# Banded attention: the sink as one more column of the logits, and every second block's result in a bank of the projections

## The chip, the cores and the metric

The kernel runs on one core of a Trainium2 chip. The metric is the device time of one execution in microseconds (us). The engines of the core work side by side, each through its own queue in order, and wait for one another by semaphores: TensorE (PE, with its weight loads as PEld), VectorE (DVE), ScalarE (ACT), GpSimd (POOL) and SyncE (SP), which here issues the DMAs.

## The reference, cut to what matters

The program is a trunk of four residual layers: a gated convolution, forgetting attention, gated DeltaNet, and sliding-window attention with sinks. Only the last one is touched. It has 16 query heads of 64 in 4 groups, a window of 128 tokens, and for every head one learned sink that takes part in the softmax and has no value:

```python
s = einsum('bnqhgd,bnkhd->bnhgqk', qb, kk) / sqrt(d)     # a block of 128 queries, 256 keys
logits = where(mask, s, -inf)
m = maximum(max(logits, -1), sink)
e = exp(logits - m)
p = e / (sum(e, -1) + exp(sink - m))
o = einsum('bnhgqk,bnkhd->bnqhgd', p, vv)
return (o * silu(z)) @ w_out
```

## The kernel before

Everything is float32, and the products are made of a high and a low part (`hi`, `lo`), so that a projection of 128 columns by 512 tokens is 8 times 3 matmuls (`proj_steps`, L158 to L160) into one PSUM bank.

PSUM has eight banks, given out by `psum(tag)`: three that rotate under the tag "pj" (each new tile takes the next of the three, and waits until the readers of the tile before it in that bank are through), two under "tr", two under "sc" and one under "ov".

`layer_swa` runs the attention as 64 blocks: 8 groups g (two heads each) times 8 blocks i of 128 queries; block n is g = n // 8, i = n % 8. TensorE's order is written out by hand (`manual_schedule`); the other engines' orders come from the scheduler. In step n of the loop TensorE does the logits of block n (`ps_sc`), the transposes of block n - 2 (`ps_tr`, L1164) and the product with the values of block n - 3 (L1173, `ps_ov`, 4 matmuls), and between these three it is filled with projections for the next group (`window`, `slot`): queries in two halves, the gate in two halves, and in group 3 also keys. So about two steps carry one projection. In group 7 the filling is the output projection.

One block (`swa_block`) goes through the engines like this:

- DVE, twice: logits plus band mask, with a running minimum that starts at the negated sink (L1150; logits are kept negated, so the minimum is the negated maximum).
- ACT, twice: exponential with its sum (L1153).
- The sink: DVE adds minimum and sink (L1155), ACT takes the exponential (L1156), DVE adds it to the sums (L1157). All three are on tiles of 128 by 2.
- DVE: reciprocal (L1158); POOL: logits times reciprocal (L1159).
- PE: transposes (L1164); ACT: high part `phi` (L1167); DVE: low part `plo` (L1168).
- PE: values (L1173) into `ps_ov`; ACT copies two quarters of it (L1177, L1178), DVE adds the other two (L1179, L1180), which frees the bank; DVE multiplies into `y` (L1183).

A projection's bank is freed by its readers: for queries by the copy `ra` on ACT (L957), after which SP swaps halves of heads by four DMAs into `acc` (L960), POOL and DVE rotate (L961 to L963), and ACT and DVE split the result into `qst` (L1012, L1017, L1019); for a gate by a tanh on ACT (L289) and the product on DVE (L290).

Of the kernel before, what the change touches and what calls it, by code (L numbers as in the profile page):

```python
# [21 lines left out]
P = 128  # L22
# [23 lines left out]
class Core:  # L46
# [286 lines left out]
    def start(self, layer, wsrc, st):  # L333
# [33 lines left out]
        def arrive(half, c):  # L367
            if c >= NC_:
                return
            if c not in pts[half]:  # L370
                pts[half][c] = self.psum("sc", 2) if c % 3 < 2 else self.psum("ov")
                for b in range(4):
                    turn(half, b, c)
            nc.scalar.copy(self.Y[c][half], pts[half][c])

        with self.tc.manual_schedule(engines={E.PE, E.Activation, E.DVE}):
# [16 lines left out]
            self.pre = [[self.split_w(raw, P, nc.vector) for raw in raws[:2]]]  # L393
            for c in range(1, AHEAD):
                arrive(0, c)
            self.pre.append([self.split_w(raw, P) for raw in raws[2:3]])
            for half in range(NH):
                lows = []
                for c in range(NC_ + 1):
                    if c < NC_:  # L400
# [530 lines left out]
def layer_swa(k, out):  # L931
    nc = k.nc
    w_in = k.a["swa_w_in"][0]
    with k.tc.tile_pool(name="sw", bufs=1) as p:
        tab = [[p.tile([P, HT], F32, name=f"rt{j}_{h}") for h in range(NH)] for j in range(2)]
        for h in range(NH):
            for j in range(2):
                nc.sync.dma_start(out=tab[j][h], in_=k.rope[j][h])
        sk = p.tile([P, 2, 16], F32, name="sk")
        nc.sync.dma_start(out=sk[:, 0, :], in_=k.a["swa_sinks"][0].partition_broadcast(P))  # L940
        nc.vector.tensor_scalar(sk[:, 1, :], sk[:, 0, :], -1.0, None, op0=ALU.mult)

        band = p.tile([P, 2 * P], F32, name="band")
        nc.gpsimd.memset(band, 0.0)
# [22 lines left out]
        vv = [p.tile([P, 4, P], F32R, name=f"vv{b}") for b in range(8)]  # L967
# [104 lines left out]
        with k.tc.manual_schedule(engines={mybir.EngineType.PE}):  # L1072
# [20 lines left out]
            for n in range(64 + 4):  # L1093
                g, i = n // 8, n % 8
# [29 lines left out]
def swa_block(k, p, g, i, q, kk, vv, sk, band):  # L1124

    nc = k.nc
    kv = g // 2
    qsl = slice((i % 4) * P, (i % 4 + 1) * P)
    kbs = [i - 1, i] if i else [0]
    n = len(kbs) * P  # L1130
    ps = k.psum("sc", 2).rearrange("p (u n) -> p u n", u=2)
    lg = p.tile([P, HT], F32, name="lg", bufs=3).rearrange("p (u n) -> p u n", u=2)
    st = k.small.tile([P, 4, 2], F32, name="st", bufs=6)

    runs = []
    for kb in kbs:
        if runs and runs[-1][0] == kb // 4:
            runs[-1][2] += P
        else:
            runs.append([kb // 4, (kb % 4) * P, P])  # L1140
    for u in range(2):
        at = 0
        for h, k0, w in runs:
            kh, kl = kk[g // 4, h]
            nc.tensor.matmul(ps[:, u, at:at + w], q[u][:, qsl], kh[kv % 2][:, k0:k0 + w], start=True, stop=False)
            nc.tensor.matmul(ps[:, u, at:at + w], q[u][:, qsl], kl[kv % 2][:, k0:k0 + w], start=False, stop=True)  # L1146
            at += w
    for u in range(2):
        hd = 2 * g + u
        nc.vector.tensor_tensor_reduce(lg[:, u, :n], ps[:, u, :n], band[:, 2 * P - n:], 1.0, sk[:, 1, hd:hd + 1],  # L1150
                                       ALU.add, ALU.min, st[:, 0, u:u + 1])
    for u in range(2):
        nc.scalar.activation(lg[:, u, :n], lg[:, u, :n], AF.Exp, bias=st[:, 0, u:u + 1], scale=-1.0,  # L1153
                             accum_out=st[:, 1, u:u + 1])
    nc.vector.tensor_tensor(st[:, 2, :], st[:, 0, :], sk[:, 0, 2 * g:2 * g + 2], op=ALU.add)  # L1155
    nc.scalar.activation(st[:, 2, :], st[:, 2, :], AF.Exp)  # L1156
    nc.vector.tensor_tensor(st[:, 2, :], st[:, 2, :], st[:, 1, :], op=ALU.add)  # L1157
    nc.vector.reciprocal(st[:, 3, :], st[:, 2, :])  # L1158
    nc.gpsimd.tensor_tensor(lg[:, :, :n], lg[:, :, :n], st[:, 3, :].unsqueeze(2).broadcast_to([P, 2, n]), op=ALU.mult)  # L1159
    yield  # L1160
    pt = k.psum("tr")
    for j in range(len(kbs)):
        for u in range(2):
            nc.tensor.transpose(pt[:, (2 * j + u) * P:(2 * j + u + 1) * P], lg[:, u, j * P:(j + 1) * P], k.ident)  # L1164
    hi = p.tile([P, HT], F32R, name="phi", bufs=2)
    lo = p.tile([P, HT], F32R, name="plo", bufs=2)
    nc.scalar.copy(hi[:, :2 * n], pt[:, :2 * n])  # L1167
    nc.vector.tensor_tensor(lo[:, :2 * n], pt[:, :2 * n], hi[:, :2 * n].bitcast(F32), op=ALU.subtract)  # L1168
    yield
    ov = k.psum("ov")  # L1170
    for j, kb in enumerate(kbs):
        for x in (hi, lo):
            nc.tensor.matmul(ov[:, :256], vv[kb][:, kv, :], x[:, j * 256:(j + 1) * 256],  # L1173
                             start=(j == 0 and x is hi), stop=(j == len(kbs) - 1 and x is lo))

    o = p.tile([P, P], F32, name="o", bufs=3)
    nc.scalar.copy(o[0:64, 0:P], ov[64:128, 0:P])  # L1177
    k.mark = nc.scalar.copy(o[64:128, 0:P], ov[0:64, P:2 * P])  # L1178
    nc.vector.tensor_tensor(o[0:64, 0:P], ov[0:64, 0:P], o[0:64, 0:P], op=ALU.add)  # L1179
    nc.vector.tensor_tensor(o[64:128, 0:P], ov[64:128, P:2 * P], o[64:128, 0:P], op=ALU.add)  # L1180
    yield
    y = k.Y[g][i // 4][:, qsl]
    nc.vector.tensor_tensor(y, y, o[:, 0:P], op=ALU.mult)  # L1183
    yield "end"


class Gdn:
# [146 lines left out]
    def decay(self, hd, h):  # L1334
# [111 lines left out]
    def loads(self, hd, h):  # L1446
# [9 lines left out]
        for q in range(4):  # L1456
# [429 lines left out]
```

## Time and profile before

| | us |
|---|---|
| median of 3 runs | 2175.01 (2165.24 to 2175.88) |
| the profiled execution | 2172.09 |
| its span on the core | 2170.4 |
| TensorE busy in the span | 2086.8 (96%) |
| VectorE busy | 1347.4 (62%) |
| ScalarE busy | 993.1 (46%) |
| GpSimd busy | 838.4 (39%) |

The shares are means over four layers with different limits. The blocks of the attention run from about 1735 to 2090 us of the span; what the change is worth is read there. A busy TensorE may be busy at half its clock: the granted clock stands beside it in the view by stretches.

### The profile page before, as it was taken

The numbers are of one execution on the slowest core, as the hardware profiler recorded it, in microseconds if no ns is written. First come the engines' busy times: TensorE is split into PE (matmuls) and PEld (weight loads), VectorE is DVE, ScalarE is ACT, GpSimd is POOL, SyncE is SP. The second block draws the span as 40 slices with busy tenths as digits, with TensorE's granted clock in tenths as the row PEclk, the third lists the DMA queues.
The fourth block names the chain that finished last, engine by engine and source line by source line (L and its number), as shares of the span: only waits on it lengthen the run. The fifth ranks groups of instructions, "written<-read, shape, count | busy, mean of one in ns | idle before, by whom it ended". The sixth has DMA issues, their size and how long they took to land.

```text
span 2170.4 us, 33535 instructions
## 1 busy us (share of the span) xinstructions
PE 2086.8 (96%) x11717; PEld 1753.5 (81%) x11717; DVE 1347.4 (62%) x2876; ACT 993.1 (46%) x2483; POOL 838.4 (39%) x721
## 2 busy tenths in 40 slices
PE   7999999999999999999999799999999998998898
PEld 6887888788988989888687677888887797877788
DVE  8647645544535353655456967765557658898874
ACT  6333334424333343543365444343444356666664
POOL 2344445631212212236366643223326544453630
PEclk9999999999999999999999999999999999999999
DMA  6122215731222312136266453333316421111134
GB/s 234 49 73 88 58 54 160 212 62 50 40 40 40 49 43 42 49 123 181 64 188 185 136 167 104 85 110 91 102 56 199 141 65 38 44 52 40 44 91 143
DMA packets 288367, 205.71 MB, mean 95 GB/s; under 512 B 41381, under 2 KB 245574, under 8 KB 288198
## 3 DMA queue, kind: packets, MB, share of 16 engines
q1 hardware_dynamic: 288198, 203.56, 33.4%
q8 instruction: 93, 1.52, 0.3%
q14 instruction: 76, 0.62, 0.1%
HBM read 154.87 MB, written 43.38 MB: 91 GB/s over the span
## 4 chain that ended last, share of the span: by engine, by line
PE 71%; DVE 14%; DMA 5%; issue 4%; ACT 3%; POOL 2%; SPq 1%; ACTq 0%; POOLq 0%; DVEq 0%
PE ps_pj L158 14%; PE ps_pj L159 14%; PE ps_pj L160 14%; PE ps_sc L247 2%; PE ps_sc L249 2%; PE ps_sc L248 2%; DVE sp L1428 1%; PE ps_tr L834 1%; DVE cu L1307 1%; PE ps_pj L247 1%; PE ps_pj L248 1%; PE ps_pj L249 1%; PE ps_pj L742 1%; PE ps_pj L744 1%; PE ps_pj L743 1%
## 5 line engine op out<-in xcount | busy, mean ns | idle before, releaser
L158 PE MATMUL ps_pj<-hhi,whi 128*128 128x512 f32 (+1 forms) x1712 | 699.7, 410 | 1.6 <-DVE y L460 0.8
L159 PE MATMUL ps_pj<-hlo,whi 128*128 128x512 f32 (+1 forms) x1712 | 670.9, 392 | 7.2 <-DVE hlo L415 3.8
L160 PE MATMUL ps_pj<-hhi,wlo 128*128 128x512 f32 (+1 forms) x1712 | 670.7, 392 | 0.4 <-DVE wlo L142 0.4
L142 POOL TENSOR_TENSOR wlo<-wraw,whi 128x512 fp32r<-128x512 f32 x296 | 406.4, 1379 | 635.6 <-ACT whi L141 594.5
L160 PEld LDWEIGHTS ps_pj<-hhi,wlo 128*128 128x128 f32 x1712 | 322.6, 188 | 69.9 <-DVE wlo L142 0.8
L159 PEld LDWEIGHTS ps_pj<-hlo,whi 128*128 128x128 f32 x1712 | 323.8, 189 | 62.1 <-DVE hlo L415 5.8
L158 PEld LDWEIGHTS ps_pj<-hhi,whi 128*128 128x128 f32 x1712 | 323.5, 189 | 57.7 <-issue 2.6
L141 ACT CAST whi<-wraw 128x512 fp32r<-128x512 f32 x304 | 186.0, 617 | 323.5 <-PE ps_pj L159 177.8
L1307 DVE SCALAR_TENSOR_TENSOR cu<-cb,taps,cu 128x512 f32<-128x512 f32 x144 | 134.4, 934 | 11.8 <-ACT cu L1305 10.1
L1159 POOL TENSOR_TENSOR lg<-lg,st 128x512 f32<-128x512 f32 (+1 forms) x64 | 64.0, 999 | 120.1 <-DVE st L1158 77.3
L887 ACT ACTIVATE lg<-lg,mx 128x512 f32<-128x512 f32 (+2 forms) x96 | 58.7, 612 | 63.9 <-DVE mx L882 63.7
L839 ACT CAST phi<-ps_tr 128x512 fp32r<-128x512 f32 (+1 forms) x80 | 40.6, 544 | 94.5 <-PE ps_tr L834 94.5
L1153 ACT ACTIVATE lg<-lg,st 128x256 f32<-128x256 f32 (+1 forms) x128 | 62.8, 491 | 45.5 <-DVE st L1150 43.8
L460 DVE TENSOR_TENSOR y<-ps_pj,xr 128x512 f32<-128x512 f32 x56 | 38.5, 688 | 63.6 <-PE ps_pj L160 56.1
L840 DVE TENSOR_TENSOR plo<-ps_tr,phi 128x512 fp32r<-128x512 f32 (+1 forms) x80 | 49.6, 634 | 42.5 <-ACT phi L839 42.5
L468 DVE TENSOR_TENSOR acc<-acc,hf 128x512 f32<-128x512 f32 x49 | 49.4, 1008 | 41.8 <-ACT hf L467 41.8
L142 POOL TENSOR_TENSOR wlo<-wr,whi 128x512 fp32r<-128x512 f32 x36 | 48.0, 1332 | 59.4 <-ACT whi L141 55.2
L1428 DVE TENSOR_TENSOR sp<-sT,sU 128x504 f32<-128x504 f32 (+18 forms) x80 | 56.9, 712 | 6.4 <-DMA sU<-gLT 5.2
L1150 DVE CUSTOM_DVE_ANT_0 lg<-ps_sc,band,sk 128x256 f32<-128x256 f32 (+1 forms) x128 | 55.0, 465 | 6.4 <-PE ps_sc L1146 4.8
L1173 PE MATMUL ps_ov<-phi,vv 128*128 128x256 f32 x120 | 33.6, 299 | 24.9 <-DVE o L1180 24.2
L290 DVE SCALAR_TENSOR_TENSOR y<-y,ps_pj 128x512 f32<-128x512 f32 x48 | 32.7, 680 | 38.1 <-ACT y L289 38.0
L742 PE MATMUL ps_pj<-whi,hhi 128*128 128x256 f32 x192 | 54.8, 285 | 0.0
(442 smaller groups left out, 4676.3 us busy)
## 6 DMA issues: line engine op xcount, KB each, us to landing
xd<-y SPq DMA_DIRECT2D x64, 256.0 KB, 3.4
wraw<-in_fox_w_in_dram SPq DMA_DIRECT2D x60, 256.0 KB, 4.2
xr<-xd SPq DMA_DIRECT2D x56, 256.0 KB, 3.0
wraw<-in_gdn_w_in_dram SPq DMA_DIRECT2D x52, 256.0 KB, 3.7
wraw<-in_conv_w_in_dram SPq DMA_DIRECT2D x40, 256.0 KB, 2.9
wraw<-in_swa_w_in_dram SPq DMA_DIRECT2D x40, 256.0 KB, 3.1
wraw<-in_conv_w_out_dram SPq DMA_DIRECT2D x32, 256.0 KB, 4.7
wraw<-in_fox_w_out_dram SPq DMA_DIRECT2D x32, 256.0 KB, 3.0
```

What stands on the lines that cost most here:

```text
L141: nc.scalar.copy(hi[:, :, :cols], raw[:, :, :cols])
L142: (eng or nc.gpsimd).tensor_tensor(lo[:, :, :cols], raw[:, :, :cols], hi[:, :, :cols].bitcast(F32), op=ALU.subtract)
L158: nc.tensor.matmul(o, hi, xhi, start=(c == 0), stop=False)
L159: nc.tensor.matmul(o, hi, xlo, start=False, stop=False)
L160: nc.tensor.matmul(o, lo, xhi, start=False, stop=(c == NC_ - 1))
L247: nc.tensor.matmul(ps, whi[:, c, :], xhi, start=start and c == 0, stop=False, skip_group_check=True)
L248: nc.tensor.matmul(ps, whi[:, c, :], xlo, start=False, stop=False, skip_group_check=True)
L249: nc.tensor.matmul(ps, wlo[:, c, :], xhi, start=False, stop=stop and c == 3, skip_group_check=True)
L742: nc.tensor.matmul(ps, xhi, whi, start=(c == 0), stop=False)
L1159: nc.gpsimd.tensor_tensor(lg[:, :, :n], lg[:, :, :n], st[:, 3, :].unsqueeze(2).broadcast_to([P, 2, n]), op=ALU.mult)
L1307: eng.scalar_tensor_tensor(u, cb[:, j:j + HT], tap(j), u, op0=ALU.mult, op1=ALU.add)
L1428: nc.vector.tensor_tensor(v, T[:, n0:i, n0:n1].rearrange("p j n -> p n j"), U[:, n0:i, i].unsqueeze(1).broadcast_to([P, n, m]), op=ALU.mult)
```

## The change

The sink becomes one more column of the logits tile. The tile `lg` gets rows of `LW` = 260 floats for each of the two heads where it had 256; ACT copies the negated sinks of the two heads into column n (one copy of 128 by 2 a block), and the exponential runs over n + 1 columns, so that its sum holds the sink's term. The three small operations L1155, L1156 and L1157 go. And the product with the values of the blocks with odd i in groups 0 to 6 goes into a tile of the tag "pj" instead of "ov".

```diff
-    lg = p.tile([P, HT], F32, name="lg", bufs=3).rearrange("p (u n) -> p u n", u=2)
-    st = k.small.tile([P, 4, 2], F32, name="st", bufs=6)
+    lg = p.tile([P, 2 * LW], F32, name="lg", bufs=3).rearrange("p (u n) -> p u n", u=2)
+    st = k.small.tile([P, 3, 2], F32, name="st", bufs=6)
...
+    nc.scalar.copy(lg[:, :, n:n + 1], sk[:, 2 * g:2 * g + 2].unsqueeze(2))
...
-        nc.scalar.activation(lg[:, u, :n], lg[:, u, :n], AF.Exp, bias=st[:, 0, u:u + 1], scale=-1.0,
+        nc.scalar.activation(lg[:, u, :n + 1], lg[:, u, :n + 1], AF.Exp, bias=st[:, 0, u:u + 1], scale=-1.0,
                              accum_out=st[:, 1, u:u + 1])
-    nc.vector.tensor_tensor(st[:, 2, :], st[:, 0, :], sk[:, 0, 2 * g:2 * g + 2], op=ALU.add)
-    nc.scalar.activation(st[:, 2, :], st[:, 2, :], AF.Exp)
-    nc.vector.tensor_tensor(st[:, 2, :], st[:, 2, :], st[:, 1, :], op=ALU.add)
-    nc.vector.reciprocal(st[:, 3, :], st[:, 2, :])
-    nc.gpsimd.tensor_tensor(lg[:, :, :n], lg[:, :, :n], st[:, 3, :].unsqueeze(2).broadcast_to([P, 2, n]), op=ALU.mult)
+    nc.vector.reciprocal(st[:, 2, :], st[:, 1, :])
+    nc.gpsimd.tensor_tensor(lg[:, :, :n], lg[:, :, :n], st[:, 2, :].unsqueeze(2).broadcast_to([P, 2, n]), op=ALU.mult)
...
-    ov = k.psum("ov")
+    ov = k.psum("pj" if g < 7 and i % 2 else "ov")[:, 0:256]
```

`sk` now holds the negated sinks alone (it held both). One line more at the head of the file and two in `swa_block` move the numbers: L159 to L161 in the changed kernel are L158 to L160 before, L958 is L957, L963 and L964 are L962 and L963, L1013 is L1012, L1018 and L1020 are L1017 and L1019, L291 is L290, L1153 is L1150, L1156 is the exponential L1153, L1150 is the new copy; from L1164 to L1183 the numbers agree, and the reciprocal keeps L1158.

TensorE's order is the same instruction for instruction; only the bank changes. This is TensorE in the changed kernel around the values of block 3 (group 0, i = 3); the tiles carry their numbers, which rise in the order in which they are given out.

```order
L159 MATMUL ps_pj_17513<-hhi7_1_90,whi_17318 128x512
L160 MATMUL ps_pj_17513<-hlo7_1_106,whi_17318 128x512
L161 MATMUL ps_pj_17513<-hhi7_1_90,wlo_17319 128x512
L1164 MATMUL ps_tr_17597<-ident_139,lg_17454 128x128 x4
L159 MATMUL ps_pj_17636<-hhi0_0_75,whi_17626 128x512
L160 MATMUL ps_pj_17636<-hlo0_0_91,whi_17626 128x512
L161 MATMUL ps_pj_17636<-hhi0_0_75,wlo_17627 128x512
L159 MATMUL ps_pj_17636<-hhi1_0_77,whi_17626 128x512
L160 MATMUL ps_pj_17636<-hlo1_0_93,whi_17626 128x512
L161 MATMUL ps_pj_17636<-hhi1_0_77,wlo_17627 128x512
L1173 MATMUL ps_pj_17643<-phi_17556,vv2_16773 128x256
```

The rows of "pj" tiles here are, in the order given out, 17513 (a projection), 17520 (values of block 1), 17636 (the next projection) and 17643 (values of block 3). With three banks in rotation 17643 takes the bank of 17513, whose last matmul stands ten rows ahead.

On ScalarE, in group 4 before, from the cast of a weight to the high part of block 37:

```order
L141 CAST whi<-wraw 128x512
L1012 CAST qst<-ra 64x512 x2
L957 ACTIVATE ra<-ps_pj 128x512
L1167 CAST phi<-ps_tr 128x512
L1153 ACTIVATE lg,st<-lg,st 128x256 x2
L1156 ACTIVATE st<-st 128x2
L1177 COPY o<-ps_ov 64x128
L1178 COPY o<-ps_ov 64x128
```

and the same place in the changed kernel:

```order
L142 CAST whi<-wraw 128x512
L1013 CAST qst<-ra 64x512 x2
L958 ACTIVATE ra<-ps_pj 128x512
L1167 CAST phi<-ps_tr 128x512
L1150 COPY lg<-sk 128x2
L1156 ACTIVATE lg,st<-lg,st 128x257 x2
L1177 COPY o<-ps_pj 64x128
L1178 COPY o<-ps_pj 64x128
```

The copy has come in ahead of the exponentials, the small exponential behind them has gone, and the copy `ra`, which frees a projection's bank, stands where it stood, behind the two casts `qst`.

On VectorE, a few blocks later in the same group, before:

```order
L963 TENSOR_TENSOR ra<-ra,acc 128x512
L1183 TENSOR_TENSOR y_1_2816<-y_1_2816,o 128x128
L1150 ISA lg,st<-ps_sc,band,sk 128x128
L1150 ISA st 128x1
L1150 ISA lg,st<-ps_sc,band,sk 128x128
L1150 ISA st 128x1
L1017 CAST hf<-ra 64x512
L290 SCALAR_TENSOR_TENSOR y_0_2818<-y_0_2818,ps_pj 128x512
```

and in the changed kernel:

```order
L1183 TENSOR_TENSOR y_1_2816<-y_1_2816,o 128x128
L964 TENSOR_TENSOR ra<-ra,acc 128x512
L1153 ISA lg,st<-ps_sc,band,sk 128x128
L1153 ISA st 128x1
L1153 ISA lg,st<-ps_sc,band,sk 128x128
L1153 ISA st 128x1
L291 SCALAR_TENSOR_TENSOR y_0_2818<-y_0_2818,ps_pj 128x512
L1018 CAST hf<-ra 64x512
```

The product of the gate, which frees that projection's bank, has moved ahead of a cast, and the product into `y` ahead of the rotation's sum.

## Rows read from the trace of the kernel before

**Rows 1.** The page's head and part 1: busy us of each engine, share, instructions.

```profile
span 2170.4 us, 33535 instructions
PE 2086.8 (96%) x11717; PEld 1753.5 (81%) x11717; DVE 1347.4 (62%) x2876; ACT 993.1 (46%) x2483; POOL 838.4 (39%) x721
```

**Rows 2.** View by stretches: length, busy us (instructions) PE, PEld, DVE, ACT, POOL, granted clock, DMA.

```profile
1770.00:2070.00 300.00, 275.34 (x1491) 232.37 (x1490) 258.05 (x755) 192.01 (x588) 141.66 (x116) 0.95 0.16 44
1811.00:1850.00 39.00, 35.86 (x192) 30.42 (x191) 34.16 (x106) 24.93 (x78) 17.03 (x15) 0.91 0.15 42
1851.00:1888.00 37.00, 34.85 (x197) 29.62 (x197) 31.47 (x94) 23.14 (x73) 16.61 (x14) 1.00 0.16 44
```

**Rows 3.** Waits of TensorE, 1770 to 2070 us: total us, times, longest.

```profile
PE ps_ov L1173 <- DVE o L1180: 23.7, 12, 3.5
```

**Rows 4.** Timeline of TensorE: start, us, instruction, [idle before it <- releaser].

```profile
1831.74 0.55 PE L1173 MATMUL ps_ov<-phi,vv 128*128 128x256 f32 x1 [2.96 <-DVE o L1180]
...
1869.91 0.35 PE L1173 MATMUL ps_ov<-phi,vv 128*128 128x256 f32 x1 [2.15 <-DVE o L1180]
...
2035.49 0.52 PE L1173 MATMUL ps_ov<-phi,vv 128*128 128x256 f32 x1 [3.54 <-DVE o L1180]
```

**Rows 5.** Timeline, what block 20 (values at 1869.91) waits for.

```profile
1865.48 0.58 ACT L1167 CAST phi<-ps_tr 128x512 fp32r<-128x512 f32 x1
...
1867.70 0.69 DVE L1168 TENSOR_TENSOR plo<-ps_tr,phi 128x512 fp32r<-128x512 f32 x1
...
1869.47 0.29 DVE L1180 TENSOR_TENSOR o<-ps_ov,o 64x128 f32<-64x128 f32 x1
```

**Rows 6.** Groups by line, 1685 to 2171 us: busy, mean ns | idle before.

```profile
L1155 DVE TENSOR_TENSOR st<-st,sk 128x2 f32<-128x2 f32 x64 | 17.5, 273 | 1.5
L1157 DVE TENSOR_TENSOR st<-st 128x2 f32<-128x2 f32 x64 | 17.4, 272 | 4.9 <-ACT st L1156 4.8
...
L1156 ACT ACTIVATE st<-st 128x2 f32<-128x2 f32 x64 | 12.6, 197 | 8.2 <-DVE st L1155 8.1
```

**Rows 7.** Instructions of the tile `st`, 1770 to 2090 us: ns min/median/max.

```profile
L1157 DVE TENSOR_TENSOR st<-st x62: 143/160/1110, 1771.8 to 2075.6; 128x2 f32<-128x2 f32 x62
...
L1155 DVE TENSOR_TENSOR st<-st,sk x61: 141/161/1249, 1773.2 to 2074.8; 128x2 f32<-128x2 f32 x61
```

**Rows 8.** Timeline of group 2: values of blocks 17, 19, 21, and readers of projections.

```profile
1854.48 0.58 ACT L957 ACTIVATE ra<-ps_pj 128x512 f32<-128x512 f32 x1
...
1855.16 0.27 PE L1173 MATMUL ps_ov<-phi,vv 128*128 128x256 f32 x1
...
1859.04 1.49 DVE L962 TENSOR_TENSOR acc<-acc,rt 128x512 f32<-128x512 f32 x1 [0.22 <-DMA acc<-ra]
...
1861.06 0.66 DVE L1157 TENSOR_TENSOR st<-st 128x2 f32<-128x2 f32 x1
...
1862.45 1.22 DVE L963 TENSOR_TENSOR ra<-ra,acc 128x512 f32<-128x512 f32 x1
...
1863.45 0.28 PE L1173 MATMUL ps_ov<-phi,vv 128*128 128x256 f32 x1
...
1863.71 1.25 ACT L1012 CAST qst<-ra 64x512 fp32r<-64x512 f32 x2 [1.48 <-DVE ra L963]
...
1864.98 0.60 ACT L957 ACTIVATE ra<-ps_pj 128x512 f32<-128x512 f32 x1
...
1874.82 0.27 PE L1173 MATMUL ps_ov<-phi,vv 128*128 128x256 f32 x1
...
1875.35 0.41 DVE L1017 CAST hf<-ra 64x512 fp32r<-64x512 f32 x1
1875.68 0.67 DVE L290 SCALAR_TENSOR_TENSOR y<-y,ps_pj 128x512 f32<-128x512 f32 x1
```

**Rows 9.** Timeline of group 4, block 39 and the gate ahead of it.

```profile
1973.11 0.27 PE L1173 MATMUL ps_ov<-phi,vv 128*128 128x256 f32 x1
...
1973.40 0.68 DVE L290 SCALAR_TENSOR_TENSOR y<-y,ps_pj 128x512 f32<-128x512 f32 x1
```

More of the change, by code (lines that the diff above doesn't have):

```diff
@@ L31 @@
 NB = 3
+LW = 260
 AHEAD = 6
@@ L938, in layer_swa @@
                 nc.sync.dma_start(out=tab[j][h], in_=k.rope[j][h])
-        sk = p.tile([P, 2, 16], F32, name="sk")
-        nc.sync.dma_start(out=sk[:, 0, :], in_=k.a["swa_sinks"][0].partition_broadcast(P))
-        nc.vector.tensor_scalar(sk[:, 1, :], sk[:, 0, :], -1.0, None, op0=ALU.mult)
+        sk = p.tile([P, 16], F32, name="sk")
+        nc.sync.dma_start(out=sk, in_=k.a["swa_sinks"][0].partition_broadcast(P))
+        nc.vector.tensor_scalar(sk, sk, -1.0, None, op0=ALU.mult)
         band = p.tile([P, 2 * P], F32, name="band")
@@ L1147, in swa_block @@
             at += w
+    nc.scalar.copy(lg[:, :, n:n + 1], sk[:, 2 * g:2 * g + 2].unsqueeze(2))
     for u in range(2):
         hd = 2 * g + u
-        nc.vector.tensor_tensor_reduce(lg[:, u, :n], ps[:, u, :n], band[:, 2 * P - n:], 1.0, sk[:, 1, hd:hd + 1],
+        nc.vector.tensor_tensor_reduce(lg[:, u, :n], ps[:, u, :n], band[:, 2 * P - n:], 1.0, sk[:, hd:hd + 1],
                                        ALU.add, ALU.min, st[:, 0, u:u + 1])
     for u in range(2):
-        nc.scalar.activation(lg[:, u, :n], lg[:, u, :n], AF.Exp, bias=st[:, 0, u:u + 1], scale=-1.0,
+        nc.scalar.activation(lg[:, u, :n + 1], lg[:, u, :n + 1], AF.Exp, bias=st[:, 0, u:u + 1], scale=-1.0,
                              accum_out=st[:, 1, u:u + 1])
-    nc.vector.tensor_tensor(st[:, 2, :], st[:, 0, :], sk[:, 0, 2 * g:2 * g + 2], op=ALU.add)
-    nc.scalar.activation(st[:, 2, :], st[:, 2, :], AF.Exp)
-    nc.vector.tensor_tensor(st[:, 2, :], st[:, 2, :], st[:, 1, :], op=ALU.add)
-    nc.vector.reciprocal(st[:, 3, :], st[:, 2, :])
-    nc.gpsimd.tensor_tensor(lg[:, :, :n], lg[:, :, :n], st[:, 3, :].unsqueeze(2).broadcast_to([P, 2, n]), op=ALU.mult)
+    nc.vector.reciprocal(st[:, 2, :], st[:, 1, :])
+    nc.gpsimd.tensor_tensor(lg[:, :, :n], lg[:, :, :n], st[:, 2, :].unsqueeze(2).broadcast_to([P, 2, n]), op=ALU.mult)
     yield
@@ L1169, in swa_block @@
     yield
-    ov = k.psum("ov")
+    ov = k.psum("pj" if g < 7 and i % 2 else "ov")[:, 0:256]
     for j, kb in enumerate(kbs):
         for x in (hi, lo):
-            nc.tensor.matmul(ov[:, :256], vv[kb][:, kv, :], x[:, j * 256:(j + 1) * 256],
+            nc.tensor.matmul(ov, vv[kb][:, kv, :], x[:, j * 256:(j + 1) * 256],
                              start=(j == 0 and x is hi), stop=(j == len(kbs) - 1 and x is lo))
```

## The prediction

> **What bounds the kernel now.** I read the page first: TensorE is busy 96% of the span and VectorE 62% [rows 1], but these are means over four layers, and the change touches only the attention of the last. So I cut out its blocks with the view by stretches. From 1770 to 2070 us TensorE is busy 275.34 of 300 us, VectorE 258.05 (86%), ScalarE 192, and the granted clock is 0.95 [rows 2]. Two losses stand there: 300 - 275.34 = 24.7 us in which TensorE is idle, and about 275.34 x 0.05 = 13.8 us in which it is busy at the lower of its two levels (1.2 instead of 2.4 GHz). Together 38.5 us, 1.8% of the span: more than that no edit can win in this stretch unless it takes work off TensorE, which this one does not.
>
> The view of waits then says who makes it idle: in 12 of its waits it is the product with the values, L1173, waiting for VectorE's L1180, which frees the one bank "ov", 23.7 us in all [rows 3]. The timeline shows that they are few and long (2.96, 2.15, 3.54 us), and that they fall in nearly every group on the block i = 4 [rows 4]. The clock hangs on them: the stretch of group 1 with the idle time of 2.96 us has 0.91, that of group 2 with one of 2.15 us has 1.00 [rows 2, 4]. So the level falls behind waits of about 3 us and did not behind this one of 2.15.
>
> Why it waits is in the rows of block 20: `phi` is there at 1866.06, `plo` at 1868.39, but L1180 of block 19 ends at 1869.76, and TensorE goes on at 1869.91 [rows 4, 5]. Of the wait, 1869.76 - 1868.39 = 1.37 us is the bank alone; the rest is VectorE being late.
>
> **The change part by part.** *The small operations.* VectorE loses L1155 and L1157, 64 of each. By their means that is 64 x (0.273 + 0.272) = 34.9 us [rows 6]; by their medians of 0.161 and 0.160 it is 20.5 us, since some are stretched to 1.2 us [rows 7]. I take 28 us of 258 and keep both ends. It is not on the path by itself: TensorE gets only what the late operations in front of a wait lose. The Trainium skill ("SBUF — State Buffer", section "SBUF: two separate sides") says that a VectorE operation with two SBUF inputs and a GpSimd operation that reads SBUF shut each other out for a whole instruction. By that rule the stretch is waiting for GpSimd and passes to the next such operation, and the sum would stay near 20.5 us; if it goes with the operation, 34.9. The medians and maxima above speak for the rule.
>
> *The sink's column.* ScalarE loses L1156 (64 x 0.197 = 12.6 us [rows 6]) and gets a copy of the same 128 by 2. No row shows this copy; the nearest is L1156 itself, so I put it at the same 12.6 us and the net at 0, between -12.6 (a free copy) and +12.6 (twice the price). ScalarE is busy 192 of 300 us, which hides either. What ScalarE no longer does is wait for L1155 between exponentials and copies, 8.1 us in all [rows 6]; but the rows behind it there wait for other things too, so I count none of it for TensorE. If the copy were late, the exponentials behind it would be, then the reciprocal and GpSimd's product; it follows the cast `phi`, whose transposes free the same tile, so I expect no wait. The wider exponential is one column in 256, nothing. GpSimd's product has gaps between its rows now, with as many elements: nothing, and its 141.66 of 300 us leave room.
>
> *The second bank.* TensorE's order does not change. Blocks with even i now wait for L1180 two blocks back instead of one, which in the rows of block 20 was over long before. So their wait shrinks to `plo`: of 2.15 us at block 20, 0.8 would be left, and less with the small operations gone. I count the waits of even blocks as gone, the 24.7 us with them.
>
> But the blocks with odd i now take a bank of the projections. The rotation runs projection, values, projection, values over three banks, so the bank of a block's values is that of the projection which ended just before, with four transposes and six matmuls between. Whoever reads that projection must be through, and here the trace lets me measure how late the readers are. In group 2:
>
> - i = 1: the reader L957 ends at 1854.48 + 0.58 = 1855.06, the values start at 1855.16 [rows 8]. No wait.
> - i = 3: L957 ends at 1864.98 + 0.60 = 1865.58, the values start at 1863.45: 2.13 us late [rows 8]. L957 stands behind the two casts `qst`, these behind L963, L962 and the DMAs of the query half before. From one L957 to the next are 10.5 us (the five groups 0, 1, 2, 4, 5 have 10.4 to 10.5), from values to values 8.3. Of the 10.5 the change takes L1157, here 0.66 [rows 8]. I count 1.5 us left.
> - i = 5: L290 ends at 1875.68 + 0.67 = 1876.35, the values start at 1874.82: 1.53 us late [rows 8]. The cast of 0.41 goes behind it, but if block 20 no longer waits 2.15 us, TensorE comes earlier by what i = 3 did not wait, 2.15 - 1.5. So 1.53 - 0.41 + 0.65 = 1.8, less the small operations on the way: 1.6 us.
> - i = 7: in group 4 L290 ends at 1973.40 + 0.68 = 1974.08, the values start at 1973.11: 0.97 late [rows 9]; 0.6 after the change.
>
> That is 3.7 us a group, 18.5 for five. Group 3 has six projections and its odd values fall later behind them, group 6 is disturbed at its end; I put them at 2.5 and 4 us, estimates below and about at the plain groups' 3.7. Together 25 us of new waits in place of 24.7. They are shorter, however: 1.5 and 1.6 us where there were 2.15 to 3.54. So I expect most of the clock's 13.8 us back, and leave a third, 5 us.
>
> **The sum.** 38.5 - (25 + 5) = 8.5 us won of the profiled execution's 2172.1: 2163.6. That execution lies 2.9 us under the median of the runs, 2175.0; I add two of these and forecast 2166 us. With small operations at the low end (20.5 us) each odd wait loses 0.2 us less, some 4 us in all: 2170; with the high end and all clock back 2157. The forecast's own range is 2157 to 2171.
>
> **The rivals.**
>
> *All waits go, 2145 us.* VectorE's load falls from 86% to about 77%, the readers come earlier by more than I count, and most of the 38.5 us is won, say 28. For it: the reader at i = 1 is already in time, and the late ones hang on VectorE. Against it: from L957 to L957 are 10.5 us against 8.3, and only 0.66 of the missing 2.2 goes. The Trainium skill ("Perfetto Trace Analysis", section "Matmuls") asks that independent groups rotate through different banks, so that the reading of one overlaps the next group's matmuls; by this rule alone this rival would be the forecast. The trace agrees for even blocks, and the lateness above stands against it for odd ones.
>
> *Slower, 2188 us.* The place is the odd block's L1173 on a "pj" bank, the price the lateness as the trace has it now, 2.13 + 1.53 + 0.97 = 4.6 us a group, some 31 us with groups 3 and 6, and the clock: two drops a group instead of one, each costing what group 1 lost, 35.86 x 0.09 = 3.2 us, in six groups say 20. That is 51 against 38.5, so 13 more, 2185 to 2188. It decides if the waits at i = 3 and i = 5 reach the length behind which the clock fell, near 3 us; at 2.15 it did not. TensorE's shorter even waits push it this way, since it comes earlier to a reader that has not become earlier.
>
> *No change, 2174 us.* The waits of odd blocks cancel those removed, and the clock stays as it is; VectorE's saved time is swallowed behind GpSimd.
>
> **Chances and range.** The forecast 0.40, all waits go 0.17, slower 0.15, no change 0.28. About 0.5% (11 us) is what a measurement of this kernel can tell from no change. The forecast lies 9 us under the median, so a little under half of it counts as faster: 0.17 + 0.19 + 0.04 from the edge of "no change" make 0.40. Slower by over 0.5% is nearly all of that rival and a little of "no change": 0.15. The rest is 0.45. The range from 2150 to 2184 leaves out most of the first rival and half of the slower one, 2 in 10.
>
> **What would show it.** Right: no wait of an even block's L1173 above 1 us; new waits of L1173 on "ps_pj" at i = 3 and i = 5, for ScalarE's `ra` and VectorE's L290 (L291 there), of 1 to 2 us; about 25 us of idle TensorE in the stretch; a granted clock of 0.97 to 0.99 there; VectorE some 28 us less busy. Wrong: if TensorE's idle time falls under 12 us (then the readers were not what I think), or if the clock stays at 0.95 with waits near 2 us, or if the even blocks still wait for L1180.

## The result, and the profile after

The changed kernel takes 2152.24 us (median of 4 runs, 2149.09 to 2152.88), the kernel before beside it 2173.25. The ratio is 0.990, 95% interval 0.988 to 0.992: 21 us faster. The forecast of 2166 had the sign and 7 of these 21 us; the range held the median by 2 us, and by luck, as the part on the prediction shows. What came was close to the rival "all waits go, 2145 us".

The profiled execution took 2149.09 us. Its page, part 1, against [rows 1]:

```profile
span 2147.4 us, 33391 instructions
PE 2078.8 (97%) x11717; PEld 1748.3 (81%) x11717; DVE 1323.6 (62%) x2748; ACT 992.1 (46%) x2483; POOL 836.8 (39%) x721
```

VectorE is 23.8 us less busy, ScalarE 1.0. The view by stretches, against the first row of [rows 2] (columns as there), and under it the stretch from the values of block 0 to those of block 55, which holds the same work in every kernel:

```profile
1770.00:2070.00 300.00, 289.12 (x1608) 243.87 (x1607) 253.01 (x673) 206.51 (x625) 149.63 (x123) 0.99 0.19 52
...
1776.41:2027.44 251.03, 244.09 (x1370) 207.28 (x1368) 217.10 (x578) 173.62 (x532) 129.27 (x106) 0.99 0.17 47
```

In the kernel before, the second of these stretches is:

```profile
1774.48:2051.61 277.13, 252.47 (x1370) 212.78 (x1368) 242.63 (x699) 178.55 (x541) 132.30 (x108) 0.96 0.16 44
```

The same 1370 matmul rows take 277.13 - 251.03 = 26.1 us less: TensorE's idle time goes from 24.66 to 6.94 us (17.7), its busy time from 252.47 to 244.09 (8.4) with the granted clock at 0.99 instead of 0.96. So the whole gain lies here (the span lost 23.0 us; elsewhere some 3 go the other way). The waits of TensorE after, from 1770 to 2050 us, against [rows 3] (either window ends some 20 us behind the values of block 55):

```profile
PE ps_ov L1173 <- DVE plo L1168: 6.4, 6, 2.1
PE ps_pj L1173 <- DVE plo L1168: 1.7, 2, 1.1
PE ps_ov L1173 <- ACT phi L1167: 0.5, 1, 0.5
```

The waits for L1180 are gone, and none for a reader of a projection has come. What is left is for `plo`, and it now stands ahead of the second matmul (`plo,vv`), not of the first: four of the eight at i = 4 (0.82 to 1.03 us), the longest at block 30 in group 3. Two of those waits, blocks 20 and 30, against [rows 4]:

```profile
1862.81 0.39 PE L1173 MATMUL ps_ov<-plo,vv 128*128 128x256 f32 x1 [0.98 <-DVE plo L1168]
...
1919.38 0.50 PE L1173 MATMUL ps_ov<-plo,vv 128*128 128x256 f32 x1 [2.06 <-DVE plo L1168]
```

And the place of the readers, block 19 (i = 3), against [rows 8]:

```profile
1857.38 0.28 PE L1173 MATMUL ps_pj<-phi,vv 128*128 128x256 f32 x1
...
1859.33 0.60 ACT L958 ACTIVATE ra<-ps_pj 128x512 f32<-128x512 f32 x1
```

The reader L958 ends at 1859.93, 2.55 us behind the start of the values: at least as late as I had measured it (2.13 us before), and TensorE did not wait. So the values cannot stand in the bank that it reads. The addresses of the tiles in the built program say the same. The "pj" tiles in the order given out, P a projection, V the values of an odd block, with their banks:

```
before:               P 5  P 4  P 3  P 5  P 4  P 3  P 5 ...
after, group 0:       P 5  P 4  V 3  P 5  V 3  P 4  V 3 ...
after, group 6:       P 4  V 5  P 3  V 5  P 4  V 5  P 3 ...
```

The sentence ahead of the prediction that 17643 takes the bank of 17513 is wrong: 17513 is the first P in bank 4, 17643 the second V in bank 3. The three banks do not go round here once tiles with other lives are among them. The values of odd blocks share one bank (3 up to group 3, 5 from there on), and the projections take turns in the other two.

The groups of the touched lines, against [rows 6] (columns as there):

```profile
L1150 ACT COPY lg<-sk 128x2 f32<-128x2 f32 x61 | 11.7, 191 | 0.1
...
L1183 DVE TENSOR_TENSOR y<-y,o 128x128 f32<-128x128 f32 x64 | 40.8, 638 | 1.5
...
L1158 DVE RECIPROCAL st<-st 128x2 f32<-128x2 f32 x64 | 10.2, 159 | 17.1 <-ACT lg L1156 16.9
```

The copy costs 191 ns against the 197 of the exponential that went: ScalarE's net is nothing, as assumed. The reciprocal now waits for ScalarE, 16.9 us in all, where before it stood behind L1157, which waited 4.8 [rows 6]. For comparison, L1183 and L1158 of the kernel before:

```profile
L1183 DVE TENSOR_TENSOR y<-y,o 128x128 f32<-128x128 f32 x64 | 35.2, 550 | 0.8
...
L1158 DVE RECIPROCAL st<-st 128x2 f32<-128x2 f32 x64 | 10.4, 163 | 1.5
```

### The profile page after: what moved, and what is told of

The parts are those of the page before. It is cut to its first block, busy times and chain, and to the rows that moved or that the text cites. A ratio compares the mean times of both kernels' runs of the same rounds, so it can differ in the third digit from the quotient of the medians.

```text
span 2147.4 us, 33391 instructions
## 1 busy us (share of the span) xinstructions
PE 2078.8 (97%) x11717; PEld 1748.3 (81%) x11717; DVE 1323.6 (62%) x2748; ACT 992.1 (46%) x2483; POOL 836.8 (39%) x721
## 4 chain that ended last, share of the span: by engine, by line
PE 74%; DVE 13%; ACT 4%; DMA 4%; issue 3%; POOL 1%; SPq 0%; ACTq 0%; POOLq 0%; DVEq 0%
PE ps_pj L159 15%; PE ps_pj L160 15%; PE ps_pj L161 15%; PE ps_sc L248 2%; PE ps_sc L250 2%; PE ps_sc L249 2%; PE ps_pj L248 1%; PE ps_pj L249 1%; PE ps_pj L250 1%; PE ps_tr L835 1%; DVE sp L1428 1%; DVE cu L1307 1%; DVE lg L1153 1%; PE ps_pj L743 1%; PE ps_pj L745 1%
## 5 line engine op out<-in xcount | busy, mean ns | idle before, releaser
L159 PE MATMUL ps_pj<-hhi,whi 128*128 128x512 f32 (+1 forms) x1712 | 698.8, 409 | 3.5 <-ACT hhi L411 1.4
L160 PE MATMUL ps_pj<-hlo,whi 128*128 128x512 f32 (+1 forms) x1712 | 669.2, 391 | 7.2 <-DVE hlo L416 3.9
L161 PE MATMUL ps_pj<-hhi,wlo 128*128 128x512 f32 (+1 forms) x1712 | 669.0, 391 | 0.0
L161 PEld LDWEIGHTS ps_pj<-hhi,wlo 128*128 128x128 f32 x1712 | 321.8, 188 | 68.9
L160 PEld LDWEIGHTS ps_pj<-hlo,whi 128*128 128x128 f32 x1712 | 323.3, 189 | 61.6 <-DVE hlo L416 5.1
L159 PEld LDWEIGHTS ps_pj<-hhi,whi 128*128 128x128 f32 x1712 | 323.1, 189 | 59.7 <-issue 2.5
L1159 POOL TENSOR_TENSOR lg<-lg,st 128x512 f32<-128x512 f32 (+1 forms) x64 | 63.7, 996 | 122.7 <-DVE st L1158 117.3
L1156 ACT ACTIVATE lg<-lg,st 128x257 f32<-128x257 f32 (+1 forms) x128 | 63.1, 494 | 49.2 <-DVE st L1153 49.0
L461 DVE TENSOR_TENSOR y<-ps_pj,xr 128x512 f32<-128x512 f32 x56 | 38.5, 687 | 64.0 <-PE ps_pj L161 57.5
L1153 DVE CUSTOM_DVE_ANT_0 lg<-ps_sc,band,sk 128x256 f32<-128x256 f32 (+1 forms) x128 | 55.0, 464 | 5.0 <-PE ps_sc L1148 3.4
L291 DVE SCALAR_TENSOR_TENSOR y<-y,ps_pj 128x512 f32<-128x512 f32 x48 | 32.7, 681 | 38.6 <-ACT y L290 38.6
L744 PE MATMUL ps_pj<-wlo,hhi 128*128 128x256 f32 x192 | 54.6, 285 | 0.0
```

The costliest lines, as they stand in the source:

```text
L159: nc.tensor.matmul(o, hi, xhi, start=(c == 0), stop=False)
L160: nc.tensor.matmul(o, hi, xlo, start=False, stop=False)
L161: nc.tensor.matmul(o, lo, xhi, start=False, stop=(c == NC_ - 1))
```

## The experiments

The question is where the 14 us came from that I had not counted. The theories (A, B, C, and later V, R, S) are defined in the expectations; C is my prediction. Each kernel was timed beside the kernel before, and the ratio is to that. Two tables collect them. The first has the runs, and from the profile the stretch from the values of block 0 to those of block 55 (length, TensorE idle in it, granted clock):

| kernel | median, us | ratio (95%) | stretch | idle | clock |
|---|---|---|---|---|---|
| before | 2173 to 2176 | 1 | 277.1 | 24.7 | 0.96 |
| bank alone | 2172.1 | 0.9987 (0.9975 to 0.9999) | 272.3 | 24.0 | 0.99 |
| sink's column alone | 2163.1 | 0.9940 (0.9924 to 0.9956) | 260.6 | 17.9 | 1.00 |
| changed, again | 2153.2 | 0.9892 (0.9875 to 0.9910) | 250.2 | 7.4 | 1.00 |
| last projection's bank | 2169.1 | 0.9967 (0.9956 to 0.9978) | 271.8 | 22.3 | 0.97 |
| own bank | 2151.8 | 0.9893 (0.9874 to 0.9911) | 250.2 | 7.3 | 1.00 |
| two additions back | 2156.9 | 0.9913 (0.9898 to 0.9929) | 254.5 | 9.8 | 1.00 |
| and a free exponential | 2161.5 | 0.9942 (0.9928 to 0.9955) | 257.0 | 10.6 | 0.99 |
| and the trip by ScalarE | 2168.2 | 0.9967 (0.9956 to 0.9979) | 263.7 | 14.7 | 0.99 |
| y on GpSimd | 2149.2 | 0.9881 (0.9862 to 0.9899) | 247.4 | 6.1 | 1.00 |
| y on GpSimd, before | 2170.5 | 0.9979 (0.9968 to 0.9990) | 271.9 | 24.7 | 0.98 |
| y on GpSimd, one bank | 2155.0 | 0.9911 (0.9894 to 0.9927) | 254.8 | 10.6 | 0.99 |

The second has the time from one block's values to the next, worked out from the timelines, by the later block's i, mean over groups 1, 2, 4 and 5 (us; undisturbed it is 4.2 to 4.5; the whole group is all eight intervals):

| kernel | i = 3 | 4 | 5 | 6 | 7 | whole group |
|---|---|---|---|---|---|---|
| before | 4.24 | 7.00 | 6.07 | 4.50 | 4.28 | 38.74 |
| bank alone | 4.14 | 4.15 | 6.85 | 4.49 | 5.50 | 37.80 |
| sink's column alone | 4.16 | 5.51 | 4.35 | 5.24 | 4.33 | 36.27 |
| changed, again | 4.17 | 4.16 | 5.34 | 4.51 | 4.35 | 35.41 |
| last projection's bank | 5.68 | 4.27 | 5.31 | 4.61 | 4.43 | 37.07 |
| two additions back | 4.17 | 4.17 | 5.59 | 4.51 | 4.64 | 35.74 |
| and the trip by ScalarE | 4.17 | 4.30 | 6.39 | 4.52 | 4.43 | 36.94 |
| y on GpSimd | 4.17 | 4.17 | 4.29 | 4.52 | 5.29 | 35.11 |

**The bank alone** (the kernel before and this line; the values' matmul drops its own slice of `ov`):

```diff
-    ov = k.psum("ov")
+    ov = k.psum("pj" if g < 7 and i % 2 else "ov")[:, 0:256]
```

> The kernel before with only the bank of the odd blocks' values changed; the sink is computed as before. Theory A (the values of odd blocks in effect have a second bank of their own, and TensorE then waits for the block's plo instead of the results of the block before): plo ends about 1.4 us ahead of those results in the waits of before, so of the 24 us of waits some 8 to 12 are left, all on plo, none on a projection's reader; VectorE as busy as before (1347 us); granted clock 0.98 to 0.99 in the stretch; 2155 to 2162 us, ratio 0.992 to 0.995. Theory B (the lighter VectorE is what gained, the bank only little): ratio 0.997 to 1.000. Theory C (my prediction: values wait for a projection's readers): 23 to 27 us of waits at i = 3 and 5, on the scaled copy and the gate's product, ratio 0.997 to 1.003.

Measured: 0.9987, nearly nothing. TensorE's waits, 1770 to 2050 us, and blocks 19 and 20 in its timeline:

```profile
PE ps_ov L1173 <- DVE plo L1168: 15.4, 12, 1.9
PE ps_tr L1164 <- POOL lg L1159: 5.9, 9, 1.9
PE ps_pj L1173 <- DVE plo L1168: 1.7, 1, 1.7
```

```profile
1863.71 0.27 PE L1173 MATMUL ps_pj<-phi,vv 128*128 128x256 f32 x1
...
1867.85 0.28 PE L1173 MATMUL ps_ov<-phi,vv 128*128 128x256 f32 x1
...
1869.27 0.69 DVE L1168 TENSOR_TENSOR plo<-ps_tr,phi 128x512 fp32r<-128x512 f32 x1
...
1870.01 0.39 PE L1173 MATMUL ps_ov<-plo,vv 128*128 128x256 f32 x1 [1.88 <-DVE plo L1168]
```

The first matmul no longer waits, and TensorE stands 1.88 us at the second instead. The waits for L1180 have become waits for `plo`, 17.1 us, and for GpSimd's product ahead of the transposes, 5.9: 24.7 us idle before, 24.0 after. From block 19's values to the start of block 20's `plo` it is 4.25 us before (1863.45 to 1867.70 [rows 5, 8]) and 5.56 here (1863.71 to 1869.27): TensorE is earlier by 1.3 us, VectorE is not. A was wrong on the size: it counted on 8 to 12 us of waits left. The ratio is what B and C gave, but no reader of a projection is among the waits, which is against C.

**The sink's column alone** (the changed kernel with `ov = k.psum("ov")[:, 0:256]`).

> The changed kernel with the values of every block in the one bank as before, so only the sink's column is left of the change. VectorE 24 to 28 us less busy than before (1320 to 1324 us). Theory A: the waits for the results of the block before stay (10 to 13 of them), each shorter by what VectorE no longer does in that block (0.4 to 0.9 us), so 14 to 20 us of waits are left, the clock stays at 0.95 to 0.97, ratio 0.995 to 0.998. Theory B: the waits go nearly as in the changed kernel, ratio 0.990 to 0.992. Theory C gives the same as A.

Measured: 0.9940, between A and B. The waits are still for the results of the block before, 17.9 us in 14 where there were 23.7 in 12 [rows 3]. At i = 4 they are 0.31 to 1.30 us; the longest, 4.1, is at block 55, the end of the stretch:

```profile
PE ps_ov L1173 <- DVE o L1180: 17.9, 14, 4.1
```

Bank 0.0013 and sink 0.0060 make 0.0073 of the whole 0.0100 to 0.0108: the bank is worth 3 us on the kernel before, and some 10 us once the sink's operations are gone. In the same way the sink's column is worth 13 us with one bank and 0.0095, some 20 us, with two.

The sink's column also brings another order on VectorE. In the traces from 1775 to 2040 us the product into `y` (L1183) stands behind the rotation's sum (L963, L964) at 11 of 13 places in the kernel before and with the bank alone, and at 5 of 13 here and in the changed kernel; the gate's product (L290, L291) stands ahead of the cast at 1 of 6 places there, and at 5 of 6 here. No run has the new column with the old order, so how much of its worth is the order is not shown.

**The last projection's bank.** The projections go round strictly (`psum("pj")` now moves on in the list `ring`) and the odd values take the bank that I had assumed:

```diff
+        k.kept["ring"] = [k.psum("pj") for _ in range(3)]
...
-    ov = k.psum("pj" if g < 7 and i % 2 else "ov")[:, 0:256]
+    ov = (k.kept["ring"][-2] if g < 7 and i % 2 else k.psum("ov"))[:, 0:256]
```

> The changed kernel, with what my prediction assumed made true by hand: the projections rotate strictly over the three banks and the values of an odd block take the bank of the projection before the one that runs. Theory C's price, as predicted for the changed kernel: new waits at i = 3 and 5 on the scaled copy (L958's line) and the gate's product, 20 to 27 us of TensorE idle in the stretch, clock 0.97 to 0.98, 2160 to 2170 us, ratio 0.994 to 0.998 to before. Theory A says that the changed kernel is faster than this one by those waits; if it is as fast as the changed kernel (ratio 0.989 to 0.991), the readers' lateness costs nothing even where it gates.

Measured: 2169 us, as C gave. The waits (L1180 here is L1173, L962 is L958, L295 is L291), and block 19:

```profile
PE ps_pj L1180 <- DVE y L295: 14.5, 8, 5.0
PE ps_pj L1180 <- ACT ra L962: 7.5, 5, 2.1
```

```profile
1865.70 0.60 ACT L962 ACTIVATE ra<-ps_pj 128x512 f32<-128x512 f32 x1
...
1866.35 0.39 PE L1180 MATMUL ps_pj<-phi,vv 128*128 128x256 f32 x1 [1.89 <-ACT ra L962]
```

22.0 us of waits by the mechanism that I had priced at 25. The total hides two misses that offset each other: in the five plain groups it is 11.1 us where I had 18.5 (the gate's waits at i = 5 are 0.7 us in the mean instead of 1.6, those at i = 7 nearly nothing), in groups 3 and 6 it is 5.0 and 5.9 instead of 2.5 and 4. It costs 16 us, and the changed kernel does not have it.

**Own bank.** The allocation of the built program written out:

```diff
+        k.kept["vb"] = k.psum("pj")
+        k.kept["ring"] = [k.psum("pj") for _ in range(2)]
...
-    ov = k.psum("pj" if g < 7 and i % 2 else "ov")[:, 0:256]
+    ov = (k.kept["vb"] if g < 7 and i % 2 else k.psum("ov"))[:, 0:256]
```

> The changed kernel with what theory A says is in effect written out: during the window the projections take turns in two banks and the values of all odd blocks have the third. Theory A: the same as the changed kernel within 0.15%, ratio 0.989 to 0.991, no wait on a reader of a projection, some 8 us of waits on plo. Theory C: slower by waits of projections for the third bank that they no longer have, ratio 0.995 or more.

Measured: 0.9893, the same as the changed kernel, and the same waits (L1181 is L1173, L1176 is L1168):

```profile
PE ps_ov L1181 <- DVE plo L1176: 6.7, 7, 2.1
PE ps_pj L1181 <- DVE plo L1176: 1.7, 2, 1.1
```

Two banks are enough for the projections; the third was to spare.

**Two additions back.** In the changed kernel, ahead of the reciprocal:

```diff
+    nc.vector.tensor_tensor(st[:, 3, :], st[:, 0, :], sk[:, 2 * g:2 * g + 2], op=ALU.add)
+    nc.vector.tensor_tensor(st[:, 3, :], st[:, 3, :], st[:, 1, :], op=ALU.add)
```

> The changed kernel with two dummy additions of 128 by 2 on VectorE put back into every block, where the sink's two stood (the first on the minimum, the second on the sums, the result unused); ScalarE's small exponential between them stays gone. Theory V (VectorE's queue sets the pace of the blocks, the small operations' time on it is the gain): VectorE 20 to 28 us busier than in the changed kernel, its waits on plo back to 12 to 20 us, 2163 to 2172 us, ratio 0.995 to 0.999, near the bank alone. Theory R (the way by ScalarE and back, ahead of the reciprocal, was what made plo late): 2150 to 2157 us, ratio 0.990 to 0.992.

Measured: 0.9913; V falls for the most part. The two operations, by line (L1158, L1159 here):

```profile
L1158 DVE TENSOR_TENSOR st<-st,sk 128x2 f32<-128x2 f32 x64 | 18.9, 295 | 1.4
...
L1159 DVE TENSOR_TENSOR st<-st 128x2 f32<-128x2 f32 x64 | 15.7, 245 | 12.8 <-ACT lg L1156 12.3
```

By these rows they take 34.6 us, but VectorE as a whole is busy only 13.5 us longer (1337.1 against 1323.6; 16.5 against the 1320.6 of the changed kernel's second profile), and the kernel loses about 4 us. The last section says where the rest is.

**The trip by ScalarE, and a free exponential.** Between the two additions, once dependent and once on constants, then into an unused column of `lg`:

```diff
+    nc.scalar.activation(st[:, 3, :], st[:, 3, :], AF.Exp)                                          # trip
+    nc.scalar.activation(lg[:, :, n + 1:n + 2], sk[:, 2 * g:2 * g + 2].unsqueeze(2), AF.Exp)        # free
```

> The changed kernel with the two dummy additions on VectorE, and now also a dummy exponential of 128 by 2 on ScalarE between them, so that the second addition waits for ScalarE as in the kernel before (ScalarE has some 12 us more than before, of 110 idle in the stretch). Theory R (it is the way by ScalarE and back, ahead of the reciprocal, that made plo late): plo of i = 4 is late by 2 us as in the bank alone, 2163 to 2172 us, ratio 0.995 to 0.999. If ScalarE's way back costs nothing: 2155 to 2160 us, ratio 0.990 to 0.993, and the gap from the two additions to the bank alone has another cause (the order that the scheduler gives VectorE or ScalarE).

> As with the exponential put back between the two dummy additions, but the exponential now reads the constant sinks and its result is unused: the same instructions on VectorE and ScalarE, without the dependence between them. Theory R (the dependence, VectorE's addition standing behind ScalarE's exponential in its queue, costs): as with the two additions alone, 2153 to 2160 us, ratio 0.990 to 0.993. Theory S (ScalarE's 12 us more are what costs): 2165 to 2171 us, ratio 0.995 to 0.998.

Measured: 0.9967 with the trip, in R's range; 0.9942 with the free exponential, between R and S. The waits for `plo` (L1171 in both), first with the trip, then with the free exponential:

```profile
PE ps_ov L1176 <- DVE plo L1171: 11.3, 8, 2.1
PE ps_pj L1176 <- DVE plo L1171: 3.9, 5, 1.3
```

```profile
PE ps_ov L1176 <- DVE plo L1171: 9.5, 11, 2.1
PE ps_pj L1176 <- DVE plo L1171: 2.0, 2, 1.2
```

But the trip does not stand where R needs it. The second addition (L1160) and the reciprocal (L1161), first with the trip, then with the free exponential:

```profile
L1160 DVE TENSOR_TENSOR st<-st 128x2 f32<-128x2 f32 x64 | 22.3, 349 | 0.2
L1161 DVE RECIPROCAL st<-st 128x2 f32<-128x2 f32 x64 | 10.2, 159 | 13.8 <-ACT lg L1156 13.6
```

```profile
L1160 DVE TENSOR_TENSOR st<-st 128x2 f32<-128x2 f32 x64 | 15.0, 235 | 13.9 <-ACT lg L1156 13.1
L1161 DVE RECIPROCAL st<-st 128x2 f32<-128x2 f32 x64 | 10.0, 156 | 0.0
```

With the trip the scheduler put the reciprocal ahead of the second addition in all 64 blocks (in the kernel before the addition comes first in all 64, with the free exponential in 57). So VectorE never stood idle for the exponential (0.2 us in all), and the reciprocal did not wait for it: R's mechanism was not tested, though its number came. What the runs show is that the dependent form costs 0.0025 (5 us) more than the free one, 6.7 us in the stretch; by which way is open. The exponential's own time is worth 0.0029 (6 us) in the runs, but only 2.5 us in the stretch of the profile, and its groups take what those with two additions take; how much is ScalarE's load alone stays between these. From the trip to the bank alone 0.0020 is left (8.6 us in the stretch). The bank alone has two things that the dummies have not: the reciprocal needs the sum, and behind it GpSimd's product and the transposes, which wait 5.9 us there and in none of the others; and the old order on VectorE. Neither was tried by itself.

**y on GpSimd**, three times: on the changed kernel, on the kernel before, and with the sink's column but one bank.

```diff
-    nc.vector.tensor_tensor(y, y, o[:, 0:P], op=ALU.mult)
+    nc.gpsimd.tensor_tensor(y, y, o[:, 0:P], op=ALU.mult)
```

> The changed kernel with the product into y (L1183, 64 of them, 41 us of VectorE) on GpSimd. Theory V: VectorE under 80% of the stretch, the 8 us of waits on plo go to 1 to 3, 2142 to 2147 us, ratio 0.985 to 0.988. Rival: GpSimd's queue, where the product with the reciprocal now stands behind one that waits for o, gets late, TensorE's transposes wait for lg, and nothing is gained (0.989 to 0.995).

> The kernel before, with only the product into y moved from VectorE to GpSimd: neither the sink's column nor the second bank. Theory V: with 35 us less on VectorE the blocks come as close together as with the sink's column alone or closer; 2158 to 2166 us, ratio 0.992 to 0.996, though the one bank is as it was. Theory A (the one bank sets the pace): most of the waits for L1180 stay, 2169 to 2175 us, ratio 0.997 to 1.000.

> The sink's column and the product into y on GpSimd, but every block's values in the one bank. Theory V: with VectorE lighter by some 60 us the results of the block before come in time in nearly every block; TensorE waits 3 to 10 us for them, 2147 to 2156 us, ratio 0.988 to 0.992: the second bank is then worth less than the 11 us that it adds to the sink's column. Theory A: the second bank keeps its worth, 2156 to 2162 us, ratio 0.992 to 0.995.

Measured: 0.9881, 0.9979 and 0.9911; V fails in the first two and holds in the third. In the first the ratio is at V's edge, within the noise, but the waits for `plo` are 6.5 us where V had 1 to 3. On the changed kernel, the stretch and the waits:

```profile
1781.90:2029.29 247.39, 241.34 (x1369) 206.38 (x1368) 191.48 (x524) 173.70 (x532) 155.81 (x161) 1.00 0.17 48
```

```profile
PE ps_ov L1173 <- DVE plo L1168: 5.9, 6, 1.8
PE ps_pj L1173 <- DVE plo L1168: 0.6, 1, 0.6
```

VectorE's share falls from 217.10 of 251.03 (86%) to 191.48 of 247.39 (77%), and TensorE waits nearly as long. By the second table the wait at i = 4 (seen in i = 5) is gone, and one at i = 6 (seen in i = 7) has come. On the kernel before, the waits for L1180 stay with VectorE 16 us less busy, as A gave:

```profile
PE ps_ov L1173 <- DVE o L1180: 18.7, 9, 2.8
```

So on these two kernels VectorE's share does not set the pace. With the sink's column and one bank the same edit does help (0.9940 to 0.9911, the stretch from 260.6 to 254.8 us). With y on GpSimd the second bank's worth is 0.9911 - 0.9881 = 0.003 instead of 0.005; the runs cannot tell these two apart.

**The changed kernel and y on GpSimd once more.**

> The changed kernel once more, unchanged, beside the one above on the same chip: 2149 to 2155 us, ratio 0.988 to 0.992.

> The changed kernel with the product into y on GpSimd once more, to see whether it is faster than the changed kernel (0.9892 in its last rounds): if it is, 2146 to 2150 us, ratio 0.987 to 0.989; with the waits on plo that it left (6.5 us of 8.6) no more than 3 us are to be had.

Measured: 0.9892 (0.9875 to 0.9910) and 0.9894 (0.9880 to 0.9908). The product into y on GpSimd is no gain that the runs can tell; no version here beats the changed kernel by more than the noise.

## Why the prediction was right and wrong

*What bounds the kernel: right.* The idle time of 24.7 us, nearly all of it waits for L1180, and the clock were what there was to win, and of 38.5 us 26.1 were won. (The 13.8 us are what the lower level costs; the time spent at it is about twice that.)

*The failed step: "the bank of a block's values is that of the projection which ended just before".* It was 25 of the 30 us that I left as lost. The readers are as late as I measured, and where the values do take that bank they cost 22.0 us of waits and 16 us of time; at i = 3 the waits are 2.13, 0.99, 1.89, 0.88 and 1.63 us in the five plain groups, 1.5 in the mean, the value that I gave. The other places were off, and the total of 25 was near by luck. But in the changed kernel the values have a bank of their own. I took the rotation from the kernel before, where all tiles of the tag live alike. The forecast of 2166 is near the 2169 of that other kernel. That 2152 lies in the range is luck: the new waits that the sum was made of did not come. The mark of being wrong that I had set, TensorE's idle time under 12 us, was met: 300 - 289.12 = 10.9, though the reason that I gave with it ("the readers were not what I think") is not the one. Nor did the even blocks stay under 1 us: blocks 30 and 44 wait 2.06 and 1.03.

*"I count the waits of even blocks as gone": right in the end, but not by the bank.* I said that the wait would shrink to `plo`. It does, and without the sink's column `plo` is then as late as L1180 was, since TensorE comes to it earlier (1.3 us at block 20): the bank alone leaves 24.0 of 24.7 us idle. Two things were late one behind the other, and taking the later away showed the other.

*"It is not on the path by itself" and "I count none of it for TensorE": wrong.* The sink's operations are worth 13 us with one bank and 20 with two. Put back on the changed kernel piece by piece, the two additions cost 0.0021, an exponential between them 0.0029, its dependence 0.0025, and 0.0020 is left to the bank alone; in the stretch these are 4.3, 2.5, 6.7 and 8.6 us. So VectorE's time, for which I took 28 us, is a smaller part. What the rest hangs on is not shown: the trip did not stand ahead of the reciprocal, and the new order on VectorE came with the column.

*The clock: right, with a smaller term.* 13.8 us were to be had by my estimate, the same matmuls took 8.4 less. The clock is at 0.99 in the bank alone with as much idle time as before, but no wait above 1.9 us; it is 0.97 with the last projection's bank and waits up to 5.0 us. But "behind waits of about 3 us" was read from too few of them. It fell behind 2.33 us at 1996.53 in the kernel before and behind 2.06 us at 1919.38 in the changed one, and not behind the 2.15 us of [rows 4] at 1869.91; the granted clock is the third number from the end:

```profile
1996.53 0.35 PE L1173 MATMUL ps_ov<-phi,vv 128*128 128x256 f32 x1 [2.33 <-DVE o L1180]
...
1994.00:2006.00 12.00, 9.67 (x48) 8.27 (x48) 10.90 (x34) 7.12 (x22) 3.79 (x3) 0.86 0.07 18
1866.00:1878.00 12.00, 9.85 (x55) 8.18 (x54) 10.91 (x33) 7.87 (x28) 3.81 (x3) 1.00 0.16 43
```

```profile
1916.00:1928.00 12.00, 9.44 (x44) 7.67 (x43) 11.17 (x36) 9.69 (x31) 5.27 (x5) 0.86 0.16 45
```

So the length of one wait does not tell by itself whether the clock falls.

*ScalarE's net at nothing and GpSimd's gaps at nothing: right* (191 against 197 ns; GpSimd 836.8 against 838.4 us).

*The stretched small operations.* The two ends were 20.5 and 34.9 us; 23.8 went in this profile, 26.8 in the second of the same kernel, between the ends. The rule that I named, of the Trainium skill ("SBUF — State Buffer", section "SBUF: two separate sides"), is that a VectorE operation with two SBUF inputs and a GpSimd operation that reads SBUF shut each other out for a whole instruction. The trace agrees: of the 64 L1183, the shortest of which take 0.28 us, 26 are stretched over 0.45 us before and 35 after, and all 26 and 33 of the 35 end 0.14 to 0.16 us behind the end of a GpSimd instruction beside them. L1183 rose from 550 to 638 ns in the mean with nothing changed in it. That the stretching of the removed operations passed on to it is not shown: with the last projection's bank, which lacks them too, it takes 567.

*The rule on banks.* Beside the rival of all waits, which I gave 0.17, I named the Trainium skill ("Perfetto Trace Analysis", section "Matmuls"): independent groups of matmuls should rotate through different banks. The trace agrees with it for odd blocks too, given the banks that they have (idle time 17.9 us with one bank, 6.9 with two). With the bank alone it gains next to nothing, because the wait behind the bank's was as long.

## What to carry to other kernels

Where a change gives a tile to a rotating tag with other lives in it, read the addresses in the built program before you price a wait on "the tile before it": the order of rotation seen so far need not hold. Before you remove a wait, look at what comes next in the same instruction's list (here `plo`, 1.4 us earlier): if the engine would arrive there just as early, the wait only changes its name, and two edits are worth more together than apart. A small operation can cost more than the engine's time that it takes: the same two additions cost about 4 us alone and 16 with an exponential between them that the second needs, for reasons that these runs do not separate. And where you put an operation back to test a chain, look in the trace whether it stands where the theory needs it: here the scheduler had moved the reciprocal ahead of it.

## What was not expected of the hardware

A VectorE instruction's own row does not tell what it costs VectorE: 64 additions of 128 by 2 at 295 and 64 at 245 ns added 13.5 to 16.5 us to its busy time, not 34.6. In the kernel with the two additions:

```profile
1926.04 0.16 DVE L1159 TENSOR_TENSOR st<-st 128x2 f32<-128x2 f32 x1
1926.11 0.16 DVE L1160 RECIPROCAL st<-st 128x2 f32<-128x2 f32 x1
...
1926.44 1.04 POOL L1161 TENSOR_TENSOR lg<-lg,st 128x512 f32<-128x512 f32 x1 [1.33 <-DVE st L1160]
...
1926.80 0.83 DVE L1185 TENSOR_TENSOR y<-y,o 128x128 f32<-128x128 f32 x1
```

The addition's row ends at 1926.20, but the next instruction starts at 1926.11: rows of neighbours overlap, and the busy time counts the overlap once. Over the timeline from 1735 to 2095 us some 11 of the 34.6 us lie under other rows (9 of 34.9 in the kernel before). Another 5.9 us are the product into `y` (L1185 here), which is back at 545 ns. That leaves 17.7, near the 13.5 to 16.5. The last two rows show the stretching: the product ends at 1927.63, 0.15 us behind GpSimd's instruction at 1927.48. The same product took 550 ns in the mean in the kernel before, 638 in the changed one, and 570 on GpSimd:

```profile
L1183 POOL TENSOR_TENSOR y<-y,o 128x128 f32<-128x128 f32 x64 | 36.5, 570 | 21.1 <-DVE o L1180 20.6 <-DMA acc<-ra 0.5
```
